# Moving the SBUF tiles behind the weight pool of a two-layer trunk kernel by multiples of 32 bytes

## The chip, the cores and the metric

The kernel runs on one core of a Trainium2 chip. The metric is the device time of one execution in microseconds (us), as the median over several executions.

## The reference

The reference is a decoder trunk of two layers on an input of 512 rows (the sequence) by 1024 columns, in float32. Layer 0 has one input projection that feeds a complex-diagonal state-space layer ("S5") and a mixture of dilated windowed attentions; both results go through one output projection. Layer 1 is an mLSTM mixer in chunks, with a projection in and one out. After each mixer comes a dense MLP with 4096 hidden columns:

```python
x = x + mix
h = rmsnorm(x, norm_mlp_g[layer])
x = x + jnp.square(jax.nn.relu(h @ w1)) @ w2
```

Nearly all of the arithmetic is in these projections: a matrix of weights times the 512 rows.

## The kernel before, in words

**Matmuls.** Activations are kept transposed, 128 features on the partitions by 512 rows along the free axis. Every operand of a projection is split in a high and a low part of type fp32r, and a product is made of three matmuls, high by high, high by low and low by high (`mm3`, and the loops in `prod_unit`, `v_unit` and `s5_glu`). Each of these is one matmul with a moving operand of 128 x 512 and a stationary one of 128 x 128, which a weight load (LDWEIGHTS, the row PEld of the profile) puts in place ahead of it; the load for the next matmul runs while the present one streams. There are 4,584 of them; of the 5,580 matmul instructions in the profile the others are small fp32 ones and transposes.

**Weight units.** Weights come from HBM in units of 128 x 1024 fp32 (512 KB), 219 in all, in the order of `unit_list`. `w_dma` brings a unit into a tile `wr`; `w_pump` splits it: ScalarE copies it into `wh` (line 117 is the helper `copy_act`), VectorE subtracts to make `wl` (line 93 is the helper `tt`). A unit feeds 24 matmuls, or 12 in the products of the last MLP (`prod_unit`). `w_pump` puts a unit's `wh` and `wl` into pool `wp` (two buffers each); from the first MLP on, every third unit (number modulo 3 equal to 2) goes into pool `wp2` instead (one buffer each). That is 64 of the 219 units.

Which operand moves and which stands still depends on the stage. In most projections the weights are stationary and the activations move: `hg` (normalised input, 16 slots), `y0` to `y3` (S5 output), `yh`/`yl` (attention output, at the output projection of layer 0), `sh`/`sl` (hidden layer of the first MLP), `mh`/`ml` (mLSTM output). In `v_unit` and in `prod_unit` it is the other way round: the activations `hg` or `sp` stand still and `wh`/`wl` move.

**Where the tiles lie.** A tile lies at one byte address in every partition. Pools are laid out one behind the other, in the order in which they are opened, and each tile takes a multiple of 32 bytes: constants and x (`cp`), weights (`wp`), temporaries (`tp`), then `hp` (with `hg`), and behind it pools that are opened and closed by stage: `zp` and `qkv`, the S5 pool `s5`, which gives its place to the attention outputs `at`; later `wp2`, and behind that by turns the MLP pool `mp` and the mLSTM pools `ml` and `mo`. The columns `rc2` and `nrc2` of `mlp_rows` are the last two tiles of `tp`. The start addresses follow from the tile sizes, in bytes. Every column offset that the 512-column matmuls use is a multiple of 512, so the remainder on 512 says where a tile's pieces start:

| tiles | pool | start of the first | remainder on 512 | on 64 |
|---|---|---|---|---|
| wh, wl | wp | 50528 | 352 | 32 |
| rc2, nrc2 | tp | 94272, 94304 | | |
| hg | hp | 94336 | 128 | 0 |
| y0 to y3 | zp | 127104 | 128 | 0 |
| wh, wl | wp2 | 127104 | 128 | 0 |
| yh4, yl4 ... | at | 163968 | 128 | 0 |
| sh, sl, s, sp | mp | 135296 | 128 | 0 |
| gb and others | ml | 135296 | | |
| mh, ml | mo | 194400 | 352 | 32 |

**Order and queues.** `EVEN_SEQ` and `ODD_SEQ` are written-out orders of the steps of the two mixers. A scheduler that simulates the program sets the static order of each engine's instructions. Nearly all DMAs go through one queue of SyncE; GpSimd issues those of DT and the small constants of layer 1. `s5_done` (step X of `EVEN_SEQ`) closes the S5 pool and opens `at`; `odd` opens `ml` and `mo` and then loads its constants.

Of the kernel before, what the change touches and what calls it, by code (L numbers as in the profile page):

```python
# [9 lines left out]
F32 = mybir.dt.float32  # L10
# [6 lines left out]
P = 128  # L17
# [44 lines left out]
class Trunk:  # L62
# [16 lines left out]

    def tmp(self, tag, shape=(P, T), dt=F32, bufs=2):  # L80
        return self.t(self.tp, shape, tag, dt, bufs)

    def acc(self):
        return self.t(self.ps, (P, T), "acc", F32, 4)
# [289 lines left out]
    def mlp_rows(self):  # L374
        self.tq, self.xr, self.pe, self.pv = {}, {}, {}, {}
        with self.tc.tile_pool(name="mp", bufs=1) as mp:
            self.sq = []
            p1 = None
            for m in range(32):
                z = self.proj(self.hg)  # L380
                if m == 1:
                    self.norm_cols()
                    self.rc2 = self.tmp("rc2", (P, 4), bufs=1)
                    self.nc.vector.reciprocal(out=self.rc2, in_=self.vc)
                    self.nrc2 = self.tmp("nrc2", (P, 4), bufs=1)
                    self.ts(self.nrc2, self.rc2, -1.0, ALU.mult)
                rr = self.tmp("rr")
                self.act(rr, z, AF.Relu)
                s = self.t(mp, (P, T), f"s{m}")
                self.act(s, rr, AF.Square)  # L390
                self.sq.append(s)
                if 2 <= m < 10:
                    self.x_rows(m - 2)
                if m in self.TS_AT:
                    self.t_sums(mp, self.TS_AT.index(m))
                if m > 16 and m % 2:
                    p1 = p1 or [self.psa(), self.psa()]
                    self.prod_unit(mp, 1, (m - 17) // 2, p1)
            self.prod_out(1, p1)
            for i in self.PRODS[1:]:  # L400
                accs = [self.acc(), self.acc()]
                for u in range(8):
                    self.prod_unit(mp, i, u, accs)
                self.prod_out(i, accs)
# [533 lines left out]
    def even(self):  # L938
        nc = self.nc
        self.mix, self.qk = {}, {}  # L940
        self.s5b, self.s5bt = {}, {}
        self.s5c, self.s5u, self.s5x, self.s5yl, self.s5e, self.s5z, self.yg, self.ul = {}, {}, {}, {}, {}, {}, {}, {}
        with ExitStack() as es:
            zp = self.zp = es.enter_context(self.tc.tile_pool(name="zp", bufs=1))
            qp = es.enter_context(self.tc.tile_pool(name="qkv", bufs=1))
            self.qp = [self.t(qp, (P, T), f"q{h}") for h in range(4)]
            self.kp = [self.t(qp, (P, T), f"k{h}") for h in range(4)]
            s5s = ExitStack()
            sp = s5s.enter_context(self.tc.tile_pool(name="s5", bufs=1))
            self.DT = [self.t(sp, (P, 8, P), f"DT{i}") for i in range(2)]  # L950
            for d in self.DT:
                nc.gpsimd.memset(d, 0.0)
            for k in range(KT):
                if k == self.PN:
                    self.s5_params(sp)
                self.prep(k, 0, not self.SQL)
            if self.SQL:
                for k in range(KT):
                    self.sumsq(k, 0)

            def u_proj(m):
                z = self.proj(self.hg)
                if m == 0:
                    self.norm_finish()
                ul = self.xt(4 + m % 2).rearrange("p (j k) -> p j k", j=8)
                self.mul(ul, z.rearrange("p (k j) -> p j k", j=8), self.r.rearrange("p (k j) -> p j k", j=8))
                self.ul[m] = ul
                self.s5_lift(sp, m)

            accs = []  # L970

            def v_step(u):
                if u == 0:
                    accs.extend(self.acc() for _ in range(4))
                self.v_unit(self.hg, accs, u)
                if u == 3:
                    self.V = [self.xt(4), self.xt(5), self.t(qp, (P, T), "V2"), self.t(qp, (P, T), "V3")]
                    for b in range(4):
                        self.act(self.V[b], accs[b], AF.Copy, scale=self.rc[:, b:b + 1])

            def s5_done():
                s5s.close()
                self.ap = es.enter_context(self.tc.tile_pool(name="at", bufs=1))

            def glu():
                self.s5_glu(zp)
                self.x_load((0, 1, 2, 3, 6, 7))

            fn = dict(u=u_proj, v=v_step, C=lambda q: self.s5_pow_b(sp, q), K=lambda q: self.s5_pow_c(sp, q), E=lambda q: self.s5_rot(sp, q),
                      T=lambda q: self.s5_mats(sp, q), B=lambda q: self.s5_in(sp, q), O=lambda q: self.s5_out(sp, q),  # L990
                      G=lambda q: self.s5_gelu(zp, q), a=lambda n: self.qk_a(n % 2, n // 2), b=lambda n: self.qk_b(n % 2, n // 2),
                      n=lambda n: self.qk_norm(n % 2, n // 2), r=lambda n: self.qk_rot(n % 2, n // 2),
                      h=self.att_step, X=s5_done, Y=glu)
            for step in EVEN_SEQ.split():
                fn[step[0]](*([int(step[1:])] if len(step) > 1 else []))
            self.x_load((4, 5))
            self.out_proj([self.mix[k] for k in range(8)], 1, OUT_ORDER)
# [82 lines left out]
    def odd(self):  # L1080
        nc = self.nc
        es = ExitStack()
        mp = es.enter_context(self.tc.tile_pool(name="ml", bufs=1))
        ot = es.enter_context(self.tc.tile_pool(name="mo", bufs=1))
        self.gb = self.t(mp, (8, 2), "gb")
        self.rst = self.t(mp, (8, T), "rst")
        self.cvw = self.t(mp, (P, 16, 4), "cvw")
# [312 lines left out]
```

## Time and profile before

| what | value |
|---|---|
| median of 3 runs | 1219.62 us (1218.83 to 1220.16) |
| the profiled execution, its own time | 1219.8 us |
| span of the profile | 1218.0 us |
| TensorE busy | 1197.8 us, 98% |
| TensorE weight loads busy | 969.3 us, 80% |
| VectorE busy | 737.8 us, 61% |
| ScalarE busy | 575.1 us, 47% |
| mean granted TensorE clock | 0.996 |

The span is the time from the first to the last instruction of the profiled execution; 1.8 us of its time lie around it. The shares are means over stages that differ: the first 75 us wait for VectorE and the S5 parameters, the attention has short matmuls, and the rest is long projections.

### The profile page before, as it was taken

How to read it: one execution, taken by the hardware profiler on the slowest of the kernel's cores; microseconds unless marked ns; L12 is line 12 of the kernel's file. 1: busy time of each engine (PE TensorE's matmuls, PEld its weight loads, DVE VectorE, ACT ScalarE, POOL GpSimd, SP SyncE). 2: the span in 40 equal slices, each digit the busy share in tenths (PEclk: the TensorE clock that was granted, in tenths of full speed). 3: DMA queues.
4: the chain of work that ended last, by engine and by line, in shares of the span. 5: the costliest groups of instructions: out<-in, count | busy, mean ns of one | idle time of the engine just before them, and what ended most of it. 6: DMA issues, size and time to landing. Idle time of an engine off the chain costs nothing.

```text
span 1218.0 us, 15221 instructions
## 1 busy us (share of the span) xinstructions
PE 1197.8 (98%) x5580; PEld 969.3 (80%) x5580; DVE 737.8 (61%) x1307; ACT 575.1 (47%) x1009; POOL 65.2 (5%) x120
## 2 busy tenths in 40 slices
PE   7989999999999999999999999999999999999998
PEld 5868776788888888888888888887888888888876
DVE  8799864554433344434449773874665564477796
ACT  5468777334331223332336554453354343456654
POOL 0522210000000000000010000000000000000000
PEclk9989999999999999999999999999999999999999
DMA  6434422332222323232324233321599995345654
GB/s 230 122 92 129 137 76 73 94 120 87 93 98 87 104 89 101 91 100 88 103 91 154 99 105 104 96 69 57 179 341 368 325 347 161 104 154 189 202 183 154
DMA packets 61195, 170.41 MB, mean 140 GB/s; under 512 B 15480, under 2 KB 16584, under 8 KB 61120
## 3 DMA queue, kind: packets, MB, share of 16 engines
q1 hardware_dynamic: 59904, 168.13, 42.0%
q0 software_dynamic: 1216, 1.31, 0.5%
q8 instruction: 44, 0.72, 0.2%
q14 instruction: 31, 0.25, 0.1%
HBM read 145.78 MB, written 21.53 MB: 137 GB/s over the span
## 4 chain that ended last, share of the span: by engine, by line
PE 94%; DVE 2%; POOL 1%; ACT 1%; issue 1%; DMA 0%; SPq 0%; DVEq 0%; ACTq 0%
PE acc L120 84%; PE psa L120 5%; PE psb L120 3%; PE psb L899 1%; POOL rA L544 1%; DVE wl L93 1%; ACT wh L117 0%; DVE x L93 0%; ACT hg L114 0%; DMA wr<-in_w_l 0%; PE psb L304 0%; PE psb L1207 0%; DVE hg L105 0%; DVE CG L93 0%; PE psb L650 0%
## 5 line engine op out<-in xcount | busy, mean ns | idle before, releaser
L120 PE MATMUL acc<-hg,wh 128*128 128x512 f32 x1616 | 513.1, 398 | 8.0 <-ACT hg L114 7.3
L117 ACT ACTIVATE wh<-wr 128x1024 fp32r<-128x1024 f32 x219 | 232.0, 1061 | 506.9 <-PE acc L120 415.8
L93 DVE TENSOR_TENSOR wl<-wr,wh 128x1024 fp32r<-128x1024 f32 x219 | 268.4, 1227 | 281.4 <-ACT wh L117 275.6
L120 PEld LDWEIGHTS acc<-hg,wh 128*128 128x128 f32 x1616 | 302.3, 189 | 77.0 <-ACT hg L114 7.3
L120 PE MATMUL acc<-hg,wl 128*128 128x512 f32 x808 | 320.1, 396 | 0.3 <-DVE wl L93 0.3
L120 PEld LDWEIGHTS acc<-hg,wl 128*128 128x128 f32 x808 | 152.3, 189 | 35.7 <-DVE wl L93 0.7
L120 PE MATMUL acc<-wh,sp 128*128 128x512 f32 x384 | 113.4, 394 | 0.0
L120 PE MATMUL acc<-sl,wh 128*128 128x512 f32 x256 | 100.6, 393 | 0.0
L120 PE MATMUL acc<-sh,wl 128*128 128x512 f32 x256 | 100.6, 393 | 0.0
L120 PE MATMUL acc<-sh,wh 128*128 128x512 f32 x256 | 100.6, 393 | 0.0
L120 PEld LDWEIGHTS acc<-wh,sp 128*128 128x128 f32 x384 | 72.1, 188 | 16.8
L120 PE MATMUL acc<-wh,hg 128*128 128x512 f32 x192 | 64.1, 408 | 5.0 <-ACT wh L117 5.0
L120 PE MATMUL acc<-wl,sp 128*128 128x512 f32 x192 | 68.8, 395 | 0.1
L120 PEld LDWEIGHTS acc<-sl,wh 128*128 128x128 f32 x256 | 48.0, 188 | 11.1
L120 PEld LDWEIGHTS acc<-sh,wh 128*128 128x128 f32 x256 | 48.0, 188 | 11.1
L120 PEld LDWEIGHTS acc<-sh,wl 128*128 128x128 f32 x256 | 48.0, 188 | 11.1
L93 DVE TENSOR_TENSOR tq<-tq,tq 128x1024 f32<-128x1024 f32 x32 | 39.1, 1223 | 17.5 <-DMA tq<-in_w2s 16.9
L120 PEld LDWEIGHTS acc<-wh,hg 128*128 128x128 f32 x192 | 37.0, 194 | 13.6 <-ACT wh L117 5.4
L117 ACT ACTIVATE sp<-s 128x256 fp32r<-128x256 f32 x112 | 45.1, 409 | 3.2 <-PE acc L120 1.7
L93 DVE TENSOR_TENSOR ev<-acc,r 128x512 f32<-128x512 f32 x16 | 11.1, 692 | 55.1 <-PE acc L120 55.1
L93 DVE TENSOR_TENSOR sp<-s,sp 128x256 fp32r<-128x256 f32 x112 | 43.7, 422 | 0.2 <-ACT sp L117 0.2
L120 PEld LDWEIGHTS acc<-wl,sp 128*128 128x128 f32 x192 | 36.0, 188 | 9.0 <-DVE wl L93 0.6
(317 smaller groups left out, 1495.5 us busy)
## 6 DMA issues: line engine op xcount, KB each, us to landing
wr<-in_w SPq DMA_DIRECT2D x96, 512.0 KB, 3.5
wr<-in_w_l SPq DMA_DIRECT2D x67, 512.0 KB, 3.5
tq<-in_w2s SPq DMA_DIRECT2D x32, 512.0 KB, 6.7
T<-tq SPq DMA_DIRECT2D x32, 512.0 KB, 5.2
wr<-T SPq DMA_DIRECT2D x32, 512.0 KB, 3.3
wr<-in_w2s SPq DMA_DIRECT2D x24, 512.0 KB, 4.3
x<-in_xT SPq DMA_DIRECT2D x16, 256.0 KB, 4.3
na<-scr SPq DMA_DIRECT2D x8, 256.0 KB, 3.8
```

Of the source, the lines that this page charges most:

```text
L93: return self.nc.vector.tensor_tensor(out=o, in0=x, in1=y, op=op)
L117: return self.nc.scalar.activation(o, x, AF.Copy)
L120: return self.nc.tensor.matmul(o, l, r, start=start, stop=stop)
L544: gt = lambda o, x, y, op: self.nc.gpsimd.tensor_tensor(out=o, in0=x, in1=y, op=op)
L899: self.nc.tensor.transpose(t[:, k * P:(k + 1) * P], p[:, k * P:(k + 1) * P], self.ident)
```

## The change

`rc2` and `nrc2` become the two halves of one tile of eight columns (32 bytes), where there were two tiles of 16 bytes that took 32 each. A new helper `skip` takes a tile of n bytes per partition and clears it on GpSimd. It is called with 128 as the first tile of `at`, and with 96 as the first of `ml`.

```diff
+    def skip(self, pool, n):
+        self.nc.gpsimd.memset(self.t(pool, (P, n // 4), "skip", F32, 1), 0.0)
...
-                    self.rc2 = self.tmp("rc2", (P, 4), bufs=1)
+                    rc2 = self.tmp("rc2", (P, 8), bufs=1)
+                    self.rc2, self.nrc2 = rc2[:, 0:4], rc2[:, 4:8]
                     self.nc.vector.reciprocal(out=self.rc2, in_=self.vc)
-                    self.nrc2 = self.tmp("nrc2", (P, 4), bufs=1)
                     self.ts(self.nrc2, self.rc2, -1.0, ALU.mult)
...
                 self.ap = es.enter_context(self.tc.tile_pool(name="at", bufs=1))
+                self.skip(self.ap, 128)
...
         ot = es.enter_context(self.tc.tile_pool(name="mo", bufs=1))
+        self.skip(mp, 96)
         self.gb = self.t(mp, (8, 2), "gb")
```

By the rule of the layout, all pools behind `tp` start 32 bytes lower, the outputs in `at` end up 96 bytes higher (128 less 32), and what lies in `ml` and `mo` 64 bytes higher (96 less 32). `wp` lies ahead of `tp` and stays. The remainders on 512 become: `wh`, `wl` in `wp` 352; `hg`, `y`, `sh`, `sl`, `s`, `sp` and the `wh`, `wl` of `wp2` 96; `yh`, `yl` 224; `mh`, `ml` 416. On 64 all of them are 32.

## Rows read from the trace of the kernel before

**Rows 1.** The page: busy time, share of the span and instructions of each engine.
```profile
PE 1197.8 (98%) x5580; PEld 969.3 (80%) x5580; DVE 737.8 (61%) x1307; ACT 575.1 (47%) x1009; POOL 65.2 (5%) x120
```
**Rows 2.** The page: the chain that ended last, share of the span by engine.
```profile
PE 94%; DVE 2%; POOL 1%; ACT 1%; issue 1%; DMA 0%; SPq 0%; DVEq 0%; ACTq 0%
```
**Rows 3.** Busy time by stretch: window, length, busy (instructions) per engine, clock, DMA share, GB/s.
```profile
0.00:75.00 75.00, 61.44 (x256) 48.46 (x256) 63.64 (x205) 38.03 (x85) 22.69 (x50) 0.95 0.48 157
130.00:225.00 95.00, 92.84 (x520) 66.64 (x519) 60.15 (x145) 67.56 (x150) 14.45 (x18) 0.98 0.31 88
270.00:620.00 350.00, 350.00 (x1520) 284.16 (x1519) 147.09 (x174) 110.03 (x140) 4.47 (x12) 1.00 0.30 97
880.00:1000.00 120.00, 120.00 (x541) 97.65 (x540) 68.23 (x75) 52.02 (x79) 0.00 (x0) 1.00 0.95 346
```
**Rows 4.** The same view, one weight unit per window: first MLP, layer 1's output projection, last products.
```profile
286.40:291.99 5.59, 5.59 (x26) 4.50 (x24) 2.52 (x3) 2.17 (x4) 0.00 (x0) 1.00 0.30 94
291.99:297.44 5.45, 5.45 (x26) 4.50 (x24) 2.52 (x3) 2.19 (x4) 0.00 (x0) 1.00 0.27 96
297.44:303.04 5.60, 5.60 (x26) 4.50 (x24) 2.52 (x3) 2.18 (x4) 0.00 (x0) 1.00 0.31 97
...
859.38:864.50 5.12, 5.12 (x23) 4.13 (x22) 3.18 (x4) 2.23 (x4) 0.00 (x0) 1.00 0.35 108
864.50:869.95 5.45, 5.45 (x26) 4.51 (x24) 3.18 (x4) 2.17 (x3) 0.00 (x0) 1.00 0.35 106
...
1082.74:1085.54 2.80, 2.80 (x14) 2.26 (x13) 2.80 (x7) 1.78 (x3) 0.00 (x0) 1.00 0.57 183
1085.54:1088.28 2.74, 2.74 (x13) 2.25 (x12) 2.74 (x7) 1.79 (x3) 0.00 (x0) 1.00 0.60 202
```
**Rows 5.** Groups of instructions: count, busy us, mean ns, idle before.
```profile
L120 PE MATMUL acc<-hg,wh 128*128 128x512 f32 x1616 | 513.1, 398 | 8.0 <-ACT hg L114 7.3
```
**Rows 6.** Timeline of ScalarE in the first MLP: start, us, instruction, idle before and releaser.
```profile
286.36 1.06 ACT L117 ACTIVATE wh<-wr 128x1024 fp32r<-128x1024 f32 x1 [3.39 <-PE acc L120]
291.96 1.06 ACT L117 ACTIVATE wh<-wr 128x1024 fp32r<-128x1024 f32 x1 [3.39 <-PE acc L120]
297.40 1.06 ACT L117 ACTIVATE wh<-wr 128x1024 fp32r<-128x1024 f32 x1 [3.23 <-PE acc L120]
```
**Rows 7.** Waits: engine, line, released by: us in total, times, longest.
```profile
ACT wh L117 <- PE acc L120: 415.8, 160, 6.0
...
POOL gb L1093 <- PE acc L120: 91.1, 1, 91.1
...
ACT wh L117 <- DMA wr<-in_w2s: 7.8, 7, 1.9
...
PE acc L120 <- ACT wh L117: 5.4, 3, 5.0
```
**Rows 8.** DMA issues: count, KB each, median us to landing.
```profile
wr<-in_w SPq DMA_DIRECT2D x96, 512.0 KB, 3.5
...
tq<-in_w2s SPq DMA_DIRECT2D x32, 512.0 KB, 6.7
T<-tq SPq DMA_DIRECT2D x32, 512.0 KB, 5.2
```
**Rows 9.** The chain that ended last: start, us, what; S5's last matmuls, then the last products.
```profile
175.77 3.52 PE psb L120 x32
...
1176.91 1.15 DVE wl L93
```
**Rows 10.** Timeline of GpSimd, from its last work in layer 0 into layer 1.
```profile
154.12 4.31 POOL L679 DMA_DIRECT2D DT<-dk  x8 [0.86 <-DMA dk<-y]
522.39 0.52 POOL L1024 MEMSET rr<- 8x512 f32 x1 [363.96 <-DVE sf L93]
614.05 0.55 POOL L1093 DMA_DIRECT2D gb<-in_gb  x1 [91.15 <-PE acc L120]
...
617.30 0.12 POOL L1094 MEMSET pw<- 128x4 f32 x1
```

## The prediction

> **What bounds the kernel now.** I began with the busy shares and the chain of waits: TensorE is busy 98% of the span [rows 1] and makes up 94% of the chain that ended last [rows 2]. Then the stretches: the first 75 us and the attention (130 to 225 us) have idle time of TensorE, the long stretches behind them have none, and there its clock is granted in full [rows 3]. So the time is the number of matmuls times the interval from one to the next, and the only question is whether the change alters that interval. The mean duration of one matmul, 398 ns, doesn't tell it, since matmuls overlap [rows 5]. I therefore took windows that hold one weight unit each [rows 4]; in their counts, 26 are the unit's 24 matmuls and two that reach in over the border.
>
> In the first MLP the units take 5.60, 5.59 and 5.45 us, in turn of three. The short one is the third unit, whose weights lie in `wp2`; the work of VectorE and ScalarE is the same in all three (2.52 and 2.17 to 2.19 us). What differs is the place. With weights in `wp` (remainder 352 on 512) and the moving `hg` at 128, the starts are 224 bytes apart; in `wp2` (128) they are 0 apart. That it isn't the pool as such is seen in layer 1's output projection, where the moving `mh` lies at 352: there a unit from `wp` takes 5.45 us, and one from `wp2` is slow (5.12 us for 22 matmuls, 233 ns each). And it holds with the roles exchanged: in the last products the weights move and `sp` stands still; 12 matmuls take 2.80 us from `wp` and 2.74 us from `wp2` [rows 4]. So a matmul during which the next weights are loaded from a start that differs by 224 bytes, either way, goes at 5.60 / 24 = 233.3 ns; with a difference of 0 it goes faster. The last matmul of a unit already runs beside the load for the following unit, so the 5.45 us hold 23 fast and one slow: (5.45 - 0.233) / 23 = 226.8 ns. The price of the difference is 6.5 ns a matmul. In the last products it is (2.74 - 0.233) / 11 = 227.9 ns, a price of 5.4. I take 6.0 for all.
>
> **The change, part by part.** *How many matmuls change class.* Units by stage, from the order of the units: layer 0's mixer 26, all from `wp`, 24 matmuls each: 624 that differ. First MLP, 64 units, 21 in `wp2`: 43 x 24 = 1,032. Layer 1's projections in, 33 units, 11 in `wp2`: 22 x 24 = 528. Its output projection, 8 units, where the two from `wp2` differ: 48. Second MLP's first matrix, 32 units, 6 in `wp2`: 26 x 24 = 624. The products: the first 8 units all fall into `wp2`; of the other 48, 16 do: 32 x 12 = 384. Together 3,240 of 4,584 differ now.
>
> After the change the differences are: 0 for everything with `wp2` (both move by 32 bytes) but 320 for `mh`/`ml`; 256 between `wp` and `hg`, `y`, `sh`/`sl`, `sp`; 128 between `wp` and `yh`/`yl`; 64 between `wp` and `mh`/`ml`. None of 64, 128, 256 and 320 occurs in the trace. *The bound from both sides:* as good as 0 (226.8 ns) or as bad as 224 (233.3 ns). I take the good end: the two slow differences seen are +224 (`wp` weights, moving `hg`) and -224 (moving `wp` weights, `sp` standing), which on 512 lie 64 apart and cost the same 233.3 ns (5.60 / 24 and 2.80 / 12) [rows 4]. A pattern that repeats every 64 bytes gives that: only half a period, 32, is slow. Then all four new differences count as 0. If they don't, a term of 96 matmuls (`yh`/`yl`: 32 + 32 + 32) and one of 192 (`mh`/`ml`, 144 of them fast now) stay or turn slow: 96 x 6.0 = 0.6 us and 192 x 6.0 = 1.2 us less gain.
>
> *Sum:* 3,240 x 6.0 = 19.4 us. Off it: in the first 75 us and in the attention TensorE waits for others [rows 3]; some 310 of the 624 lie there, and of their 1.9 us I count half, -0.9. Near the end the chain runs through a `wl` of VectorE, 1.15 us that TensorE waits for or nearly so [rows 9]; what TensorE saves in the five units ahead of it, 60 x 6.0 = 0.4 us, I count as lost. That leaves 18.1 us.
>
> *What could be late next.* TensorE would run 2.6% faster through a unit: 5.45 instead of 5.60 us. ScalarE's splitting of weights waits 3.2 to 3.4 us in each unit for TensorE to free a buffer [rows 6], 415.8 us in all, against 7.8 us for the loads of the second MLP's weights [rows 7]; 0.15 us of 3.2 is no limit. The DMAs are busiest from 880 to 1000 us, 95% at 346 GB/s, with TensorE never idle [rows 3]. Of the 541 matmuls there at most two in three differ, so TensorE would want the same bytes up to 541 x 2/3 x 6.0 = 2.2 us sooner. `w_pump` splits up to three units ahead of the running one, which is 11 us and more, so I count nothing; if that cover were gone, 2 us.
>
> *The moved operands of the other engines and DMAs.* ScalarE's copy into `wp` (32 on 64) and into `wp2` (0 on 64) takes 1.06 us either way [rows 6]: nothing. Loads into `wr` (32 on 64) land in 3.5 us; those into `tq` (0 on 64, then 32) take 6.7 us in the saturated stretch [rows 8]. Better or worse, between 0 and the same 2 us of cover.
>
> *The two memsets.* A memset of 128 x 4 takes 0.12 us on GpSimd [rows 10]; these are 24 and 32 columns, 0.1 to 0.2 us each. The one in `at` must wait until S5's last matmuls have read what lies there, 179.3 us [rows 9]; GpSimd has nothing queued between 158.4 and 522.4 us [rows 10], and nobody reads the gap. The one in `ml` goes ahead of the loads of `gb` and the others, which wait for TensorE until 614.05 us anyhow [rows 7, 10]; behind it are six small loads, `pw` and four more memsets, 0.1 us later. TensorE has two units (11 us) in hand: nothing, at most 0.1 us. *One tile for two columns:* both are written by VectorE in the same order; nothing.
>
> The profiled execution took 1219.8 us, 0.2 more than the median. 1219.8 - 18.1 = 1201.7; against the median 1201.5.
>
> **The rivals.** *A longer period (or only equal starts are fast).* Then 256 is as slow as 224, everything from `wp` stays at 233.3 ns, and 144 matmuls of `mh`/`ml` turn slow: 1219.6 + 0.9 = 1220.5 us. For it: the trace shows no other fast difference than 0. Against: the equal cost of +224 and -224. Chance 0.08.
>
> *Placement doesn't act on TensorE at all.* Then the 0.15 us between units come from something that goes with the unit, and nothing moves: 1219.6 us. The switch of roles between `wp` and `wp2` in layer 1's output projection [rows 4] speaks against it. With the tile not shrinking as I reckon it, which would leave the places alone, chance 0.04. The Trainium skill, "TensorE: Matmul & The Clock Gate", Part 2 (What happens when you issue a matmul), speaks for this rival: by it weights and moving operand come through two independent read ports, and loading the next weights takes no bandwidth from the running matmul. By that rule place is indifferent and the time stays; the trace doesn't agree, at 5.45 against 5.60 us for the same 24 matmuls.
>
> *The new differences cost more than the old one (slower).* Place: the matmuls with `wp` weights at 256, about 3,100. It decides from 233.3 + 2.4 / 3.1 = 234.1 ns on, which is 0.2% of the time. If 256 costs as much again as 224 does, 6.5 ns on top, that is 3,100 x 6.5 = 20 us: 1240 us. No unit in the trace is slower than 233.3 ns a matmul with TensorE busy throughout. Chance 0.04.
>
> **How the numbers follow.** The forecast has 0.81; 0.03 is left for a gain partly eaten by a new wait, between 1209 and 1217 us. About 0.2% (2.4 us) is what a measurement here can tell from no change. Faster by more: 0.81 + 0.03 = 0.84; within: 0.12; slower: 0.04. The range: at the low end a price of 6.5 for all and nothing hidden, 3,240 x 6.5 = 21.1, 1198.5 us; at the high end the two small terms lost (1.8), the cover of the DMAs gone (2), the price at 5.4 (-1.9) and 1 to 2 us of waits in the mixers, 1208.5 us.
>
> **What would show it.** In the profile after, units from `wp` and `wp2` both at 5.45 us for 24 matmuls in the first MLP, 2.73 us for 12 in the products, busy time of TensorE about 1180 us, and in layer 1's output projection both kinds at 227 ns. `yh`/`yl` and `mh`/`ml` tell whether 128 and 64 are as good as 0. Wrong would be: units still in turn of 5.60, 5.60, 5.45 (the longer period), or new waits of TensorE for `wh` and `wl` from 880 to 1000 us.

## The result and the profile after

The changed kernel takes 1201.56 us (1201.11 to 1202.68, 4 runs), the kernel before 1219.61 (1218.83 to 1220.16, 4 runs): a ratio of 0.9854, 95% interval 0.9837 to 0.9871. The forecast was 1201.5, in a range of 1198.5 to 1208.5.

The busy line of the page answers to [rows 1].

```profile
PE 1177.3 (98%) x5580; PEld 968.8 (81%) x5580; DVE 736.8 (61%) x1307; ACT 574.4 (48%) x1009; POOL 65.4 (5%) x122
```

The instructions are the same but for two more on GpSimd. The busy time of all engines stays within 1 us, except that of TensorE: 20.5 us less. Its weight loads are as long as before (968.8 against 969.3 us), so no shorter loads show in the profile.

Next the view by windows, one weight unit in each, with the columns of [rows 4]: three units in a row of the first MLP (the first from `wp2`, the others from `wp`), one of layer 0's output projection, two of layer 1's, and two of the last products; last the stretch in which the DMAs are busiest.

```profile
290.40:295.84 5.44, 5.44 (x26) 4.50 (x25) 2.52 (x3) 2.18 (x4) 0.00 (x0) 1.00 0.29 96
295.84:301.28 5.44, 5.44 (x26) 4.50 (x25) 2.52 (x3) 2.18 (x4) 0.00 (x0) 1.00 0.33 99
301.28:306.72 5.44, 5.44 (x26) 4.50 (x25) 2.52 (x3) 2.18 (x4) 0.00 (x0) 1.00 0.29 96
227.96:233.53 5.57, 5.57 (x25) 4.51 (x24) 3.18 (x4) 2.20 (x3) 0.00 (x0) 1.00 0.29 95
853.94:859.44 5.50, 5.50 (x26) 4.51 (x25) 3.18 (x4) 2.17 (x3) 0.00 (x0) 1.00 0.36 107
859.44:864.93 5.49, 5.49 (x26) 4.50 (x24) 3.18 (x4) 2.19 (x3) 0.00 (x0) 1.00 0.32 93
1070.91:1073.63 2.72, 2.72 (x14) 2.25 (x12) 2.72 (x7) 1.78 (x3) 0.00 (x0) 1.00 0.59 202
1073.63:1076.35 2.72, 2.72 (x14) 2.25 (x12) 2.72 (x6) 1.78 (x3) 0.00 (x0) 1.00 0.56 194
866.00:986.00 120.00, 120.00 (x551) 99.49 (x550) 69.10 (x76) 53.22 (x82) 0.00 (x0) 1.00 0.96 350
```

The pattern of three is gone: 5.44 us for every unit of the first MLP, 226.7 ns a matmul, whichever pool the weights come from. The products run at 2.72 us. But the outputs behind the two gaps don't reach that: `yh`/`yl` share their units with `y` (5.57 us), and the units of `mh`/`ml` from `wp`, which took 5.45 us before [rows 4], take 5.50 and 5.49 now. The DMA stretch asks for 350 GB/s instead of 346 [rows 3], and TensorE has no idle time in it.

The profiled execution took 1202.68 us, the longest of the four and 1.1 us above their median, with a span of 1200.9 us. By stages, from the first matmul of a unit to that of another, the 17.1 us between the spans (1218.0 less 1200.9) go like this: layer 0's mixer 256.7 us before and 255.8 after; first MLP and the gates' unit 361.8 and 354.9; the rest of layer 1's projections in 202.1 and 199.4; its output projection 54.8 and 54.8; the second MLP up to the products 204.5 and 200.5; the products 134.1 and 131.5.

The two memsets in the timeline of GpSimd, beside [rows 10]:

```profile
178.93 0.12 POOL L84 MEMSET skip<- 128x32 f32 x1 [20.91 <-PE psb L123]
...
606.14 0.12 POOL L84 MEMSET skip<- 128x24 f32 x1 [89.18 <-PE acc L123]
606.20 0.54 POOL L1098 DMA_DIRECT2D gb<-in_gb  x1
```

Each takes 0.12 us. The first waits for S5's last matmuls with nothing behind it; the second waits for what `gb` waited for before, and `gb` goes out 0.06 us after its start.

### The profile page after: what moved, and what is told of

The parts are those of the page before. It is cut to its first block, busy times and chain, and to the rows that moved or that the text cites. A ratio compares the mean times of both kernels' runs of the same rounds, so it can differ in the third digit from the quotient of the medians.

```text
span 1200.9 us, 15231 instructions
## 1 busy us (share of the span) xinstructions
PE 1177.3 (98%) x5580; PEld 968.8 (81%) x5580; DVE 736.8 (61%) x1307; ACT 574.4 (48%) x1009; POOL 65.4 (5%) x122
## 4 chain that ended last, share of the span: by engine, by line
PE 93%; DVE 3%; ACT 2%; POOL 1%; issue 1%; DMA 0%; SPq 0%; DVEq 0%; ACTq 0%
PE acc L123 83%; PE psa L123 5%; PE psb L123 3%; DVE wl L96 1%; PE psb L902 1%; POOL rA L547 1%; ACT wh L120 0%; ACT hg L117 0%; DMA wr<-in_w_l 0%; DVE hg L108 0%; PE psb L1212 0%; PE psb L307 0%; DVE x L96 0%; DVE CG L96 0%; PE psb L653 0%
## 5 line engine op out<-in xcount | busy, mean ns | idle before, releaser
L123 PE MATMUL acc<-hg,wh 128*128 128x512 f32 x1616 | 505.8, 393 | 8.9 <-ACT hg L117 8.2
L123 PE MATMUL acc<-hg,wl 128*128 128x512 f32 x808 | 316.8, 392 | 0.6 <-DVE wl L96 0.6
```

The source lines that it names most:

```text
L123: return self.nc.tensor.matmul(o, l, r, start=start, stop=stop)
```

## The experiments

Differences are given from here on as the start of the moving operand less that of the next matmul's stationary one, "on 256": as the remainder after division by 256. Before, `hg` and `wp` were 32 apart in this count, moving weights of `wp` and `sp` 224. The mean granted clock was 0.993 to 0.997 in all runs. Medians of before were 1219.2 to 1219.6 us beside each of them.

**First: the gaps without the shift.**

```diff
-                    rc2 = self.tmp("rc2", (P, 8), bufs=1)
-                    self.rc2, self.nrc2 = rc2[:, 0:4], rc2[:, 4:8]
+                    self.rc2 = self.tmp("rc2", (P, 4), bufs=1)
+                    self.nrc2 = self.tmp("nrc2", (P, 4), bufs=1)
```

> The change without its shift: rc2 and nrc2 are two tiles again, both gaps stay. Difference of starts between wp and hg, y, sh, sp is 224 again. Theory 1 (the difference of the starts of the moving operand and of the next stationary one sets the interval of the matmuls): units of the first MLP from wp at 5.60 us again, about 1220 us in all, within 1 us of before. Rival (the gaps, or a new order of the instructions, bring the gain): it stays near 1202 us.

Measured: 1219.91 us, ratio to before 1.0004 (0.9994 to 1.0013). Three units of its first MLP by windows, from `wp2`, `wp`, `wp`:

```profile
291.18:296.63 5.45, 5.45 (x26) 4.50 (x24) 2.52 (x3) 2.19 (x4) 0.00 (x0) 1.00 0.31 96
296.63:302.23 5.60, 5.60 (x26) 4.50 (x24) 2.52 (x3) 2.18 (x4) 0.00 (x0) 1.00 0.31 97
302.23:307.82 5.59, 5.59 (x25) 4.50 (x24) 2.52 (x3) 2.17 (x4) 0.00 (x0) 1.00 0.28 94
```

The old pattern is back with 32 bytes alone. The gaps and the memsets by themselves gain nothing.

**Second: the shift without the gaps** (both calls of `skip` left out).

> The shift without the gaps: attention outputs 256 from the weights in wp, mLSTM outputs 32 and 224 from them. Theory 1: mh/ml matmuls, 192, at 233 ns (229 in the changed kernel), +0.8 us; yh/yl, 96, at 227 (232 in the changed kernel), -0.4 us; about 1202.0 us. Rival A (only the remainder on 64 counts, and what mh/ml and yh/yl lose lies in their stages): yh/yl stay at 232. Rival B (the gaps bring part of the gain in other ways): 1204 us or more.

Measured: 1201.79 us. A unit of layer 0's output projection, then one of layer 1's from `wp`:

```profile
226.25:231.69 5.44, 5.44 (x26) 4.50 (x24) 3.18 (x4) 2.19 (x3) 0.00 (x0) 1.00 0.35 101
852.10:857.70 5.60, 5.60 (x25) 4.51 (x24) 3.18 (x4) 2.17 (x3) 0.00 (x0) 1.00 0.27 98
```

Without the gap `yh`/`yl` lie at 0 and their units take 5.44 us; so the 5.57 in the changed kernel came from the gap of 128, not from their stage. Without the gap of 96 `mh`/`ml` lie at 224 and take 5.60. One gap hurts by about as much as the other helps.

**Third: every difference 0.**

```diff
-                self.skip(self.ap, 128)
...
-        self.skip(mp, 96)
+        self.skip(mp, 32)
```

> The shift, no gap in at, and 32 bytes instead of 96 in ml: every difference of starts is 0 on 256. Theory 1 with a period of 256 and grades (0 best, 64 worse by 2 ns, 128 by 4 to 5, 32 and 224 by 6): mh/ml and yh/yl at 227 ns, 0.8 us less than the changed kernel, about 1200.8 us. Rival A (period 64): nothing changes, 1201.6 us, mh/ml at 229 and yh/yl at 232.

Measured: 1200.65 us (1200.35 to 1200.98). The same two kinds of unit:

```profile
226.50:231.94 5.44, 5.44 (x26) 4.51 (x24) 3.18 (x4) 2.19 (x3) 0.00 (x0) 1.00 0.33 103
851.69:857.13 5.44, 5.44 (x25) 4.50 (x24) 3.18 (x4) 2.17 (x3) 0.00 (x0) 1.00 0.30 110
```

All units are now alike, and the period of 64 falls: going from 64 to 0 takes `mh`/`ml` from 5.50 to 5.44 us.

**Fourth: `wp2` alone moved by 32 bytes** in the changed kernel.

```diff
         self.wp2 = self.ctx.enter_context(self.tc.tile_pool(name="wp2", bufs=1))
+        self.skip(self.wp2, 32)
+        self.skip(self.ctx.enter_context(self.tc.tile_pool(name="wq", bufs=1)), 480)
```

> The changed kernel with wp2 alone moved up by 32 bytes (what lies behind it moves by 512). Theory 1: the third units now take 5.60 us and the units from wp stay at 5.45, the pattern turned round; about 1,250 matmuls at 6 ns more, +7.5 us, 1209 us. Rival (absolute places or the size of the pools count, not differences): no third unit slows, 1201.6 us.

Measured: 1210.5 us, 8.9 more than the changed kernel (forecast 7.5). Units from `wp2`, `wp`, `wp`:

```profile
288.44:294.03 5.59, 5.59 (x25) 4.51 (x24) 2.52 (x3) 2.18 (x4) 0.00 (x0) 1.00 0.24 94
294.03:299.48 5.45, 5.45 (x26) 4.50 (x24) 2.51 (x3) 2.19 (x4) 0.00 (x0) 1.00 0.33 98
299.48:304.93 5.45, 5.45 (x26) 4.51 (x25) 2.51 (x3) 2.19 (x4) 0.00 (x0) 1.00 0.29 97
```

The pattern is turned round: the pool that is off is the slow one. `wp2` now lies at 128 on 512, as in the kernel before, where its units were the fast ones. So not the place counts, but the difference.

**Fifth and seventh: 64, 128, 96 and 160 in large numbers**, by gaps ahead of `hg` (64; 96), in the first MLP's pool (64; 64), in the second's (128; none) and in `ml` (480; 448) of the third experiment.

> Built on the third experiment (all differences 0 on 256, 1200.7 us), with gaps that put hg, y, yh and sp 64 from the weights in wp, and sh/sl 128 from wp and 64 from wp2 (sp 128 from wp2): on 256, about 2,990 matmuls at 64 or 192, 790 at 128. Theory 1 (grades on 256: 64 costs 2 ns, 128 costs 4.6 ns): units of the first MLP with hg from wp at 5.50 us, those with sh from wp at 5.56 us, those with hg from wp2 at 5.44; 6.0 + 3.6 = 9.6 us more, 1210 us. Rival (only the remainder on 64 counts, and mh/ml and yh/yl were slow by their stages): 1200.7 us, all units at 5.44.

> Built on the third experiment, with gaps that put hg, y and yh 96 and sh/sl and sp 160 on 256 from the weights in wp: 2,084 matmuls at 96, 1,151 at 160, 263 at 64. Theory 1 (odd multiples of 32 cost 6 to 7.5 ns, as 96 of mh/ml at 233.3 and 160 of yh/yl at 234.7 in the first experiment): 12.9 + 8.6 + 0.5 = 22 us more than 1200.7, 1222.6 us, slower than the kernel before. Rival (all odd multiples of 32 are alike, 6.1 ns): +20, 1221. Rival (cost falls towards 128): 1215 or less.

Measured: 1211.7 and 1222.09 us (ratio of the latter to before 1.0025, 1.0014 to 1.0036: slower than the kernel before). Units of the fifth: `hg` at 0, `hg` at 64, `sh`/`sl` at 128.

```profile
289.42:294.86 5.44, 5.44 (x26) 4.50 (x24) 2.52 (x3) 2.18 (x4) 0.00 (x0) 1.00 0.29 96
294.86:300.35 5.49, 5.49 (x25) 4.51 (x24) 2.51 (x3) 2.17 (x4) 0.00 (x0) 1.00 0.26 98
360.79:366.39 5.60, 5.60 (x25) 4.50 (x24) 1.23 (x1) 1.06 (x2) 0.00 (x0) 1.00 0.31 99
```

Two more windows of the fifth, both at 192: 24 matmuls of `v_unit`, where `wh`/`wl` move, and 22 of `mh`/`ml` with weights from `wp2`.

```profile
629.72:635.32 5.60, 5.60 (x26) 4.51 (x24) 2.86 (x6) 2.62 (x4) 0.00 (x0) 1.00 0.39 143
853.85:858.98 5.13, 5.13 (x24) 4.14 (x22) 3.18 (x4) 2.20 (x3) 0.00 (x0) 1.00 0.32 104
```

And of the seventh: `hg` at 96, `sh`/`sl` at 160.

```profile
297.90:303.50 5.60, 5.60 (x25) 4.50 (x24) 2.52 (x3) 2.17 (x4) 0.00 (x0) 1.00 0.31 92
364.70:370.32 5.62, 5.62 (x25) 4.52 (x24) 1.23 (x1) 1.06 (x2) 0.00 (x0) 1.00 0.27 96
```

Per matmul that is 226.7 ns at 0, 229 at 64, 233.3 at 32, 96, 128 and 192 (233.2 by the 22), 234.2 at 160. The grades on 256 hold, with two corrections. 128 costs all of the 6.7 ns and not the 4.6 that I had from `yh`/`yl`, which alternate with `y` at 0: 2.1 ns more for 790 matmuls, 1.7 us. And 192, which the forecast counted with 64, costs as much as 128, with either operand moving. The fifth came out 1.7 us above its forecast; what each of the two adds to that wasn't measured by itself.

**Sixth: `hg` 16 bytes further inside its tile.**

```diff
-            self.hgs = self.t(self.hp, (P, 16, T), "hg", F32R, 1)
+            self.hgs = self.t(self.hp, (P, 16 * T + 128), "hg", F32R, 1)[:, 4:4 + 16 * T].rearrange("p (k t) -> p k t", t=T)
```

(The attention's use of the same tile is moved likewise.)

> Built on the third experiment, with the 16 slots of hg 16 bytes further inside a wider tile and everything else in its place (modulo 512): hg, about 2,700 matmuls, 16 or 240 from the weights of both pools, all others 0. If what counts is which 32-byte piece a start falls into: 1200.7 us. If 16 is as bad as 32 (6.1 ns): +16.5 us, 1217 us, units with hg at 5.59, units with sh at 5.44. In between if the cost grows with the difference.

Measured: 1211.87 us. Units with `hg` from `wp2` and from `wp` (both at 16), then one with `sh`/`sl` at 0:

```profile
290.08:295.64 5.56, 5.56 (x26) 4.51 (x24) 2.51 (x3) 2.18 (x4) 0.00 (x0) 1.00 0.28 94
295.64:301.20 5.56, 5.56 (x26) 4.51 (x24) 2.52 (x3) 2.18 (x4) 0.00 (x0) 1.00 0.25 97
362.05:367.49 5.44, 5.44 (x26) 4.50 (x24) 1.23 (x1) 1.06 (x2) 0.00 (x0) 1.00 0.34 104
```

16 bytes cost 5.0 ns a matmul, three quarters of what 32 cost. So it isn't the 32-byte piece that counts. In `v_unit`, where `hg` stands still, the difference is 240, and 24 matmuls take 5.60 us:

```profile
629.86:635.46 5.60, 5.60 (x26) 4.54 (x24) 2.86 (x6) 3.49 (x4) 0.00 (x0) 1.00 0.30 94
```

240 costs more than 16, and 192 more than 64: a difference and its negative need not cost the same, though 32 and 224 do.

**Eighth: `wl` alone 32 bytes off**, to see which of two weights matters.

```diff
-            l = self.t(pool, (P, 1024), "wl", F32R, bufs)
+            l = self.t(pool, (P, 1024 + 128), "wl", F32R, bufs)[:, 8:8 + 1024]
```

> Built on the third experiment, with wl alone 32 bytes further in its tile (wh and all activations as there). One matmul in three then runs beside the load of a wl that lies 32 bytes off, and another one uses it. In the first MLP these have names of their own: the order is sh with wh, sl with wh, sh with wl. If the load for the next matmul counts, sl,wh is the slow one (its neighbour's wl is being loaded); if the matmul's own weights count, sh,wl. Price about 1,530 x 6 ns = 9 us either way, 1210 us; up to 1219 if a slow matmul drags its neighbours along; 1200.7 us if only wh counts.

Measured: 1225.38 us, slower than before (ratio 1.0046, 1.0029 to 1.0062) and above all that was expected. The groups of the first MLP's second matrix in the third experiment (count, busy us, mean ns, idle before):

```profile
L123 PE MATMUL acc<-sh,wh 128*128 128x512 f32 x256 | 99.6, 389 | 0.0
L123 PE MATMUL acc<-sl,wh 128*128 128x512 f32 x256 | 99.6, 389 | 0.0
L123 PE MATMUL acc<-sh,wl 128*128 128x512 f32 x256 | 99.6, 389 | 0.0
```

and in this one:

```profile
L123 PE MATMUL acc<-sl,wh 128*128 128x512 f32 x256 | 102.4, 400 | 0.0
L123 PE MATMUL acc<-sh,wh 128*128 128x512 f32 x256 | 101.1, 395 | 0.0
L123 PE MATMUL acc<-sh,wl 128*128 128x512 f32 x256 | 99.6, 389 | 0.0
```

The longest is `sl` with `wh`, whose own weights are in place and beside which the shifted `wl` is loaded; `sh` with `wl`, which uses the shifted weights, is as short as ever. The ends of matmuls are modelled in the profile, so the starts have to bear this out, and they do: in this run the next matmul starts 239.5 ns after `sl` with `wh`, 232.5 after `sh` with `wh` and 228.0 after `sh` with `wl` (means of some 256 each), in the third experiment 226.4 to 227.0 after each. So it is the load for the next matmul that counts. But the matmul ahead of it grows too, though nothing is off there. Together the three take 700 ns, and a unit 5.60 us, as if all three were off: the price isn't a sum over single matmuls.

```profile
364.85:370.45 5.60, 5.60 (x25) 4.50 (x24) 1.23 (x1) 1.06 (x2) 0.00 (x0) 1.00 0.29 98
```

Here `wl` lies 32 bytes from `wh` too, but that isn't the reason: where a unit from `wp2` follows one from `wp` in the first MLP of the kernel before, the next weights are also 32 on 256 from the present ones, and 0 from `hg`, and the next matmul starts 227 ns later by the starts in its trace.

**Ninth and tenth: the changed kernel and the third experiment once more**, side by side on one chip.

> The changed kernel again, beside the third experiment on one chip: 1201.6 us.

> The third experiment again (no gap in at, 32 bytes in ml). By its matmuls: mh/ml 183 x 1.9 ns, yh/yl 96 x 4.8, y 137 x 3.3 less than in the changed kernel, 1.3 us: 0.9 to 1.3 us below it. Rival (the first difference was chance): the same within 0.3 us.

Measured: 1201.09 us (1200.84 to 1201.38) and 1200.46 us (1200.07 to 1200.80). The ranges, of four runs each, don't overlap, but by 0.04 us only: 0.6 us here, under the 0.9 to 1.3 that were forecast, and 0.9 between the first runs. The version without the gap in `at` and with 32 bytes in `ml` is the fastest found, by less than 0.1%.

## Why the prediction was right, and where it was not

*What bounds it, and the class of the change:* right. The interval between matmuls is set by the difference between two addresses; the first, third and fourth experiments show it both ways. The rival by which place doesn't matter falls with them, and so does the one by which a longer period makes 256 slow: the period is longer, but 256 is as fast as 0. The Trainium skill, "SBUF — State Buffer", section "Who interferes with whom", has two independent read ports on TensorE and says it never waits on anyone; the runs don't agree: 5.44 against 5.60 us for a unit of `mh`/`ml` by a gap alone (third and second experiment).

*The bound taken for the four new differences:* the step that failed. I argued for a period of 64 because +224 and -224 cost the same; but two equally slow values don't fix a period, and on 256 they are simply 32 and 224. The period that the runs bear out is 256, and within it nothing measured is as good as 0. That the forecast survived is luck: 256, the difference of some 3,100 matmuls, is 0 on 256 as well as on 64. Had the shift made it 64, the same argument would have missed by 3,100 x 2.2 = 7 us, and had it made it 128 or 192, by 3,100 x 6.6 = 20 us, more than the whole gain (prices of the fifth experiment). The two small terms (128 for `yh`/`yl`, 64 for `mh`/`ml`), which I had at 0 and bounded at 0.6 and 1.2 us, turned out real: 0.7 us in layer 0's output stage (34.0 us in the changed kernel, 33.3 in the third experiment) and 0.35 in layer 1's (54.8 and 54.5).

*The sum:* the near hit of 1201.5 is luck in part, since terms were off in both directions. The price was too small. The first MLP gave 6.96 us for 1,032 x 6.0 = 6.2, the second's first matrix 4.0 for 3.7, the products 2.66 for 2.3; by whole units the price is (5.60 - 5.44) / 24 = 6.7 ns. What had pulled it down to 6.0 were the 5.4 of the products. But there the weights move, and what is loaded beside a unit's last matmul is `sp` again, so there was no slow matmul to take off the 2.74 us; 2.80 against the 2.72 of now gives 6.7 for them as well.

Against that, layer 1's projections gave 2.7 us for 3.2, for a reason that wasn't found. Layer 0's mixer was to give 2.8 (624 x 6.0 less 0.9) and gave 0.85, but most of that shortfall lies in the one execution. Its first 78 us, where others set the pace, move by more than a microsecond: the same matmul starts at 78.40 us before, at 78.70 in the changed kernel and at 76.87 in the same kernel's other profile (ninth experiment). In that one the mixer ends at 254.0 us instead of 255.8, 2.7 earlier than before. From that matmul to the mixer's end both profiles gain 1.15 us, after the 0.7 us that the gap in `at` costs there.

*What could be late next:* right. The DMA stretch held with 350 GB/s, the memsets cost nothing. The loss near the end was there: TensorE's waits for `wl` grew from 0.9 to 1.7 us in all (first the line of before, then that of after), one of them 0.40 us beside the row updates.

```profile
PE acc L120 <- DVE wl L93: 0.9, 3, 0.3
PE acc L123 <- DVE wl L96: 1.7, 4, 0.6
...
1161.69 0.74 PE L123 MATMUL acc<-wl,sp 128*128 128x512 f32 x2 [0.40 <-DVE wl L96]
```

*The slower rival* (the new differences cost more than the old): not so for 256, but it names something real. 160 costs 0.9 ns more than 32, and the seventh kernel is slower than the one before.

## What to carry to other kernels

Where TensorE is busy throughout and each 128 x 512 fp32r matmul has a new stationary operand, compare the start addresses of the moving operand and of the weights loaded next: here a multiple of 256 gave 226.7 ns a matmul, every other difference tried 229 to 234. Put padding where it makes the remainders on 256 equal for every pool that meets another, for a tile of a few bytes ahead of a big pool shifts all of them. And measure the interval by whole units of work in windows, since the mean duration of overlapping matmuls hides it.

## What was not expected

A single shifted load in three slows a neighbour too: with `wl` off by 32 a unit takes 5.60 us, as much as with every load off (eighth experiment), and in the changed kernel the units that mix `y` at 0 and `yh`/`yl` at 128 take 5.57 us, nearer to 5.60 than to the middle of 5.44 and 5.60. Why the period is 256, why 64 is cheap (5.49 us) and 128 and 192 are not, and why the matmul ahead is delayed was not settled: the runs show that the two addresses set the interval, not by what mechanism. Nor was it tried whether other shapes or types than 128 x 512 fp32r show it.
